# A decoder layer on one core: ten more chunks of the down projection by seven products, with the sums of their weights formed earlier and kept in DRAM

## The chip, the core and the metric

The kernel runs on one NeuronCore of a Trainium2 chip. The core's engines run side by side, each through its own queue in program order: PE multiplies matrices, DVE and ACT work elementwise, POOL here issues transfers and little else, SP issues the other transfers. A result goes from engine to engine by semaphores. SBUF is the memory on the core, PSUM holds PE's sums, DRAM is the large memory outside. The metric is the device time of one execution in microseconds; lower is better.

## The reference

One layer on 256 tokens of width 2048, in 32-bit floats:

```python
for l in range(DEPTH):
    h = rms_norm(x, attn_norm_g[l])
    proj = h @ w_in[l]
    q, k, v, p = jnp.split(proj, [ATTN_WIDTH, 2 * ATTN_WIDTH, 3 * ATTN_WIDTH], axis=-1)
    ...
    a = moba_attention(q, k, heads(v), rel_bias)
    m = multiscale_pool(p, pool_w[l], pool_scale[l])
    x = x + jnp.concatenate([a, m], axis=-1) @ w_out[l]
    x = x + conv_ffn(rms_norm(x, ffn_norm_g[l]), w_up[l], conv_w[l], conv_b[l], w_down[l])
```

Here `conv_ffn` multiplies by `w_up` (2048 x 11264), applies a causal convolution of width 3 to each column over the tokens, multiplies SiLU of the first half (the gate) with the second half (the value), and multiplies by `w_down` (5632 x 2048). The four large products, with `w_in` (2048 x 4096), `w_out` (2048 x 2048), `w_up` and `w_down`, are nearly all of the arithmetic.

## The kernel before, in words

**Weights and their two parts.** All weights come as a sequence of *chunks*, 128 partitions by 2048 columns, 1 MB each, in the order of their use: 24 chunks for the input projection's first part, 25 for its pooling part and the output projection, then three *thirds* of the feed-forward layer (8, 8 and 6 groups of 256 hidden columns). To keep 32-bit accuracy, a number is split into a high part, which PE multiplies at full rate, and a low part, the rest. A chunk is loaded by SP into one of four `raw` buffers (`load`, L112), ACT copies the high part into `wh` (L125, from chunk 51 on L151, one chunk further ahead), and DVE subtracts that from `raw` into `wl` (L126 or L157). A product of two matrices is then three matmuls: high by high, high by low, low by high. There are four `wh` and three `wl` buffers. When `wl` is made, the `raw` buffer is free and the chunk four further on is loaded into it (`release`, L189).

**Order of the work.** The program is a list of steps, one for each half chunk; the loop at L939 writes a step's instructions for all engines in turn. With the step that begins chunk c it first writes the splitting of chunk c + 2 (and ACT's copy of c + 3), then what was put off (`agenda`, filled by `later`; `deferred`), then the chunk's matmuls, and after a block's last matmul the evacuation of its sums. Each engine keeps this order.

**Output projection.** Eight blocks of 256 output columns, four steps (two chunks) each; the first two are mixed with the pooling weights. After a block, `residual` (L683) copies half of the sums by ACT, adds the other half by DVE (L511), adds the residual (L686) and sums squares (L691 on ACT, L692 on DVE); one step later `x2_split` makes the normalised input's two parts. After the last block, `sums2` forms the rows of mean squares, which go through DRAM on POOL's queue to be spread over the partitions. Loads of the residual `x2f` stand on SP's queue when `open_late` (L661) opens the second pool of buffers, four steps into this stage.

**Up projection.** In each third, each group has a gate block and a value block, two chunks each. After a block DVE evacuates it (L511, L767); with the next step come its convolution (L776 on ACT, L777 and L779 on DVE) and, for a value block, the product with the gate (L802). Two steps later the low part of the hidden values is made (L807), and for groups that use seven products `left_sums` (L812) forms four sums of the hidden values' quarters, split in their turn (ACT L821, DVE L822, two steps later). In the first third `x2_turn` also transposes the residual through DRAM.

**Down projection.** A chunk holds 256 hidden rows by 1024 output columns of `w_down`: a 2 x 2 matrix of blocks (128 by 512) on either side. `eight_products` takes eight products, 24 matmuls. `seven_products` uses the Strassen-Winograd scheme: seven products of sums of blocks, 21 matmuls, with the left side's sums from `left_sums` and the right side's four sums of weight blocks from `right_sums` (L163), which DVE forms in place in `raw` (L167 to L170) and ACT (L179) and DVE (L181) split into `th` and `tl`. Both halves of the output columns (`nb`) pass in turn. `SEVEN` (L55) says which groups of a third go by seven products: groups 1, 3 and 5 in the first two thirds, 1 and 3 in the last, 16 of 44 chunks.

## Time and profile before

| | |
|---|---|
| median of 3 runs | 998.84 us (998.66 to 999.5) |
| profiled execution | 999.07 us, span 997.3 us |
| granted TensorE clock | 1.000 |
| PE busy | 990.7 us, 99% |
| DVE busy | 802.1 us, 80% |
| ACT busy | 528.9 us, 53% |
| POOL busy | 61.4 us, 6% |
| moved by DMA | 210.34 MB, mean 211 GB/s |

The span runs from the first to the last instruction. Busy time of PE counts matmuls as they overlap, so it shows where PE had work and not how fast it went; the distance between the starts of two matmuls tells that. In groups of instructions a row has the line, engine, operation, the tiles written and read, the shapes and the count, and behind the bar the busy time in us and the mean of one in ns. In a timeline a row has the start and the duration in us, engine, line and tiles, and in brackets how long the engine was idle before it and what ended that.

### The profile page before, as it was taken

What the parts mean: (1) busy time and instruction counts of PE and PEld (TensorE: products, weight loads), DVE (VectorE), ACT (ScalarE), POOL (GpSimd) and SP (SyncE); (2) the same over time, 40 slices, a digit from 0 to 9 for tenths busy, and PEclk for the clock granted to TensorE, in tenths of its full rate; (3) what the DMA queues carried; (4) which work ended last, traced back from release to release, by engine and by line L of the source; (5) the groups of instructions that cost most, each with busy time, mean ns of one, the idle gap of its engine ahead of it and who ended that gap; (6) DMA issues with size and microseconds to landing.
All of it is one profiled execution on the core that took longest, in us unless ns stands there. A gap on an engine that the chain in (4) does not pass through costs nothing.

```text
span 997.3 us, 13236 instructions
## 1 busy us (share of the span) xinstructions
PE 990.7 (99%) x5306; PEld 856.8 (86%) x5306; DVE 802.1 (80%) x943; ACT 528.9 (53%) x560; POOL 61.4 (6%) x119
## 2 busy tenths in 40 slices
PE   9999999999999999999999999999999999999998
PEld 7888888898888888888888888888888888888886
DVE  6776858867779968789998778878999867877996
ACT  6554545446456555456544555555554545555641
POOL 0302232200003300000000000000000000000000
PEclk9999999999999999999999999999999999999999
DMA  9959685665558965554656555555455665555361
GB/s 351 316 208 291 233 259 195 206 261 199 195 178 284 302 218 180 193 191 166 215 207 217 206 188 192 190 197 205 163 199 186 219 235 180 192 191 208 130 237 55
DMA packets 36156, 210.34 MB, mean 211 GB/s; under 512 B 5288, under 2 KB 7720, under 8 KB 13184
## 3 DMA queue, kind: packets, MB, share of 16 engines
q1 hardware_dynamic: 31408, 197.58, 56.4%
q0 software_dynamic: 4688, 11.94, 4.2%
q8 instruction: 41, 0.67, 0.3%
q14 instruction: 19, 0.16, 0.0%
HBM read 201.23 MB, written 8.26 MB: 210 GB/s over the span
## 4 chain that ended last, share of the span: by engine, by line
PE 91%; issue 4%; DMA 3%; DVE 1%; POOL 1%; SPq 0%; ACT 0%; POOLq 0%; DVEq 0%
PE ps_feat L241 41%; PE ps_down L828 23%; PE ps_feat L243 20%; PE ps_val L219 4%; PE ps_tok L229 2%; DMA qT<-q1d 1%; DMA eT<-e3d 1%; DMA q0d<-q0x 1%; PE ps_pool L250 1%; DMA eT<-e0d 1%; DMA raw<-in_wts 0%; DVE wl L126 0%; POOL qT L441 0%; DMA e0d<-e0x 0%; PE ps_s L462 0%
## 5 line engine op out<-in xcount | busy, mean ns | idle before, releaser
L241 PE MATMUL ps_feat<-x2h,wh 128*128 128x512 f32 x1406 | 478.2, 389 | 0.0
L243 PE MATMUL ps_feat<-x2h,wl 128*128 128x256 f32 x1408 | 388.6, 276 | 0.0
L241 PEld LDWEIGHTS ps_feat<-x2h,wh 128*128 128x128 f32 x1406 | 263.9, 188 | 54.6
L157 DVE TENSOR_TENSOR wl<-raw,wh 128x2048 fp32r<-128x2048 f32 (+2 forms) x145 | 286.1, 1990 | 3.0 <-issue 3.0
L243 PEld LDWEIGHTS ps_feat<-x2h,wl 128*128 128x128 f32 x1408 | 264.3, 188 | 0.0
L151 ACT ACTIVATE wh<-raw 128x2048 fp32r<-128x2048 f32 (+2 forms) x145 | 241.3, 1677 | 39.6 <-PE ps_down L828 30.3
L828 PE MATMUL ps_down<-wh,hid 128*128 128x512 f32 x512 | 163.3, 389 | 0.0
L126 DVE TENSOR_TENSOR wl<-raw,wh 128x2048 fp32r<-128x2048 f32 (+3 forms) x60 | 119.6, 2000 | 49.6 <-ACT wh L125 40.9
L511 DVE TENSOR_TENSOR fs<-ps_feat,fs 128x512 f32<-128x512 f32 x52 | 35.9, 691 | 97.7 <-ACT fs L510 97.7
L828 PEld LDWEIGHTS ps_down<-wh,hid 128*128 128x128 f32 x512 | 96.1, 188 | 20.0
L125 ACT ACTIVATE wh<-raw 128x2048 fp32r<-128x2048 f32 (+3 forms) x60 | 99.9, 1682 | 10.8 <-DMA raw<-in_wts 7.5
L828 PE MATMUL ps_down<-wl,hid 128*128 128x512 f32 x256 | 99.6, 389 | 0.0
L241 PE MATMUL ps_feat<-cat,wh 128*128 128x512 f32 x256 | 87.3, 389 | 0.0
L229 PE MATMUL ps_tok<-wh,xh 128*128 128x512 f32 x256 | 80.0, 391 | 0.0
L510 ACT ACTIVATE fs<-ps_feat 128x512 f32<-128x512 f32 x52 | 31.0, 596 | 84.7 <-PE ps_feat L243 83.2
L243 PE MATMUL ps_feat<-cat,wl 128*128 128x256 f32 x256 | 70.7, 276 | 0.0
L179 ACT ACTIVATE th<-raw 128x1024 fp32r<-128x1024 f32 x32 | 34.0, 1063 | 51.3 <-DVE raw L168 46.0
L229 PEld LDWEIGHTS ps_tok<-wh,xh 128*128 128x128 f32 x256 | 48.0, 188 | 10.0
L828 PEld LDWEIGHTS ps_down<-wl,hid 128*128 128x128 f32 x256 | 48.1, 188 | 9.9
L241 PEld LDWEIGHTS ps_feat<-cat,wh 128*128 128x128 f32 x256 | 48.1, 188 | 9.8
L803 ACT ACTIVATE hid<-y 128x512 fp32r<-128x512 f32 x22 | 13.9, 633 | 76.7 <-DVE y L802 76.7
L229 PE MATMUL ps_tok<-wl,xh 128*128 128x512 f32 x128 | 49.8, 389 | 0.0
(196 smaller groups left out, 1076.0 us busy)
## 6 DMA issues: line engine op xcount, KB each, us to landing
raw<-in_wts SPq DMA_DIRECT2D x178, 1024.0 KB, 4.9
raw<-in_wts SPq DMA_DIRECT2D x4, 512.0 KB, 7.0
x2d<-x2x POOLq DMA_DIRECT2D x4, 512.0 KB, 6.3
x<-x2d POOLq DMA_DIRECT2D x32, 64.0 KB, 6.0
xboth<-in_xT SPq DMA_DIRECT2D x6, 256.0 KB, 10.0
out<-x SPq DMA_DIRECT2D x3, 512.0 KB, 3.9
x2f<-in_xT SPq DMA_DIRECT2D x1, 1024.0 KB, 8.7
x2f<-in_xT SPq DMA_DIRECT2D x1, 768.0 KB, 6.8
```

The source lines that it names most:

```text
L125: nc.scalar.activation(wh, w, AF.Copy)
L126: nc.vector.tensor_tensor(wl, w, wh.bitcast(F32), op=OP.subtract)
L151: nc.scalar.activation(w[:, lo:lo + n], raws[c][:, lo:lo + n], AF.Copy)
L157: nc.vector.tensor_tensor(wl[:, lo:lo + n], r[:, lo:lo + n], wh[:, lo:lo + n].bitcast(F32), op=OP.subtract)
L179: nc.scalar.activation(part(t[0]), part(r), AF.Copy)
L219: nc.tensor.matmul(ps[b][:, t, :], xh[:, k, a, ts], w[:, ws], start=False, stop=(k == KT - 1 and n == 2), skip_group_check=True)
L229: nc.tensor.matmul(ps[:, t, :], act[:, k0 + k, a, ts], w[:, ws], start=(first and k == 0 and n == 0), stop=(last and k == 1 and n == 2))
L241: nc.tensor.matmul(ps, wh[:, ws], act[:, k, :, :], start=(bool(first) and n == 0), stop=False, skip_group_check=True)
L243: nc.tensor.matmul(ps[:, S:], wl[:, ws], act[:, k, 0, :], start=False, stop=(last and n == len(ks) - 1), skip_group_check=True)
L510: nc.scalar.activation(dst, ps[:, :, S:], AF.Copy)
L511: nc.vector.tensor_tensor(dst, ps[:, :, :S], dst, op=OP.add)
L828: nc.tensor.matmul(ps, a, w, start=(first and n == 0), stop=(last and n == 2), skip_group_check=True)
```

## The change

Ten more chunks go by seven products: groups 1 to 5 in the first two thirds and 1 to 3 in the last, 26 of 44 (`SEVEN`). The right side's sums are no longer formed where they are used. For each of the 26 chunks the host lays out the blocks b22, b12, b11, b21 once more as an array `mix`. During the output projection (six) and the up projection (twenty), SP loads such a chunk into a `raw` buffer, `make` forms the four sums in place on DVE with three operations, and POOL stores the 1 MB to DRAM (`mixed`). The load that follows into that buffer is written two steps later (`later(2, load_next)`). In the down stage such a chunk then comes as two: a `sum` chunk, loaded from `mixed` (2048 columns), and a `rest` chunk with b11, b22 and b21 (1536 columns). Both are split like any other chunk, and the seven products fall into twelve matmuls (`seven_mixed`) and nine (`seven_rest`). `plan` lists the chunks in order and the places of the makes: in the output projection at chunks 40, 42, ... 50, in the up projection once per group. `th`, `tl` and their pieces are gone; the room goes to a fifth `raw` buffer (from `open_late` on) and to two more buffers for the left sums, which also hold the residual `x2f` now (four tiles, five loads). No arithmetic moves to the host, which only lays weights out.

```diff
-SEVEN = ((1, 3, 5), (1, 3, 5), (1, 3))
-TOFF, SOFF, SPAD = 32, 48, 64
+SEVEN = ((1, 2, 3, 4, 5), (1, 2, 3, 4, 5), (1, 2, 3))
+MAKES = (40, 42, 44, 46, 48, 50)
+PAIRS = ((2, 3, 4, 5, 6, 7), (0, 1, 2, 3, 4, 5, 6, 7), (0, 1, 2, 3, 4, 5))
+SOFF, SPAD = 32, 64
...
+def plan():
+
+    rows, makes = [(k, i) for i, k in enumerate(24 * ["tok"] + 25 * ["feat"])], list(MAKES)
+    n = t = 0
+    for (g0, g1), sevens, pairs in zip(THIRDS, SEVEN, PAIRS):
+        makes += [len(rows) + 4 * p + 3 for p in pairs]
...
+    mixed = [dram.tile([P, CH], F32, name=f"mixed{i}", tag=f"mixed{i}") for i in range(len(makes))]
+    order = [r for c in range(len(rows)) for r in [c] + [("make", i) for i, m in enumerate(makes) if m == c]]
+    del order[:4]
...
+        if isinstance(c, tuple):
+            src, n = mix[c[1]], CH
+        else:
+            kind, i = rows[c]
+            src, n = mixed[i] if kind == "sum" else wts[i], n or width(c)
         s = slice(lo, lo + n)
-        (queue or nc.sync).dma_start(raws[c][:, s], wts[c][:, s])
+        (queue or nc.sync).dma_start(raws[c][:, s], src[:, s])
...
-    def right_sums(r):
...
+    def make(i):
+
+        r = raws.pop(("make", i))
+        t3, t2, t4 = (r[:, k * 512:(k + 1) * 512] for k in (0, 2, 3))
+        nc.vector.tensor_tensor(r[:, :1024], r[:, :1024], r[:, 512:1536], op=OP.subtract)
+        nc.vector.tensor_tensor(t2, t3, t2, op=OP.add)
+        nc.vector.tensor_tensor(t4, t4, t2, op=OP.subtract)
+        nc.gpsimd.dma_start(mixed[i], r)
+        later(2, load_next)
...
+    def load_next():
+
+        if order:
+            c = order.pop(0)
...
             load(c)
...
-        for k0, k1 in ((0, 2), (2, 8), (8, KT)):
+        late["x2f"] = [block("x2f").rearrange("p (k t) -> p k t", t=S) for _ in range(4)]
+        for k0, k1 in ((0, 2), (2, 4), (4, 8), (8, 12), (12, KT)):
...
-    def seven_products(u, j, run, first, last):
...
+    def seven_mixed(u, j, run, first):
+
+        c = where[u][0]
+        t3, t1, t2, t4 = quarters(c)
+        del wparts[c]
+        s1, s2, s3 = (tuple(late["S", j][:, a, i, :] for a in range(2)) for i in range(3))
+        a22 = tuple(late["hid"][:, 2 * j + 1, a, P:] for a in range(2))
         p1, p5, p6, p7 = run["p"]
-        product(p5, s1, t1, first, last)
-        product(p6, s2, t2, first, last)
-        product(p7, s3, t3, first, last)
-        product(c1[0], a22, t4, (1, 0) in run["left"], False)
-        product(p1, a11, b11, first, last)
+        product(p5, s1, t1, first, False)
+        product(p6, s2, t2, first, False)
+        product(p7, s3, t3, first, False)
+        product(run["c"][1][0], a22, t4, (1, 0) in run["left"], False)
+
+    def seven_rest(u, j, run, first, last):
...
+        product(run["p"][0], a11, b11, first, last)
         product(c0[0], a12, b21, (0, 0) in run["left"], False)
         product(c0[1], s4, b22, (0, 1) in run["left"], False)
...
-            c, now[0] = u // 2 + 2, u
+            c, now[0] = starts[u] + 2, u
...
+            for i, m in enumerate(makes):
+                if m == c:
+                    make(i)
             for f in agenda.pop(u, ()):
                 f()
...
         if seven:
-            return [np.concatenate([b11, b12], axis=1), np.concatenate([b22, b21], axis=1)]
+            mix.append(np.concatenate([b22, b12, b11, b21], axis=1))
+            return [np.concatenate([b11, b22], axis=1), np.concatenate([b21, np.zeros_like(b21)], axis=1)]
```

Three places of DVE's queue show what moves (each row an instruction: line, operation, tile written from tiles read, size). The changed file's lines have other numbers: L159 and L187 are the low parts (L126 and L157 before), L195 to L197 the make, L533 an evacuation's add (L511), L788 the up block's scaling (L767), L828 the hidden values' low part (L807). First one block of the output projection, before:

```order
L511 TENSOR_TENSOR fs<-ps_feat,fs 128x512
L686 TENSOR_TENSOR x2f<-fs,x2f 128x512
L692 TENSOR_TENSOR sq_1799<-sq_1799,xs 128x512
L126 TENSOR_TENSOR wl<-raw,wh 128x2048
L702 SCALAR_TENSOR_TENSOR x2h<-x2f,pv,x2h 128x256 x2
L126 TENSOR_TENSOR wl<-raw,wh 128x2048
```

and now:

```order
L533 TENSOR_TENSOR fs<-ps_feat,fs 128x512
L707 TENSOR_TENSOR x2f<-fs,x2f 128x512
L713 TENSOR_TENSOR sq_1829<-sq_1829,xs 128x512
L159 TENSOR_TENSOR wl<-raw,wh 128x2048
L723 SCALAR_TENSOR_TENSOR x2h<-x2f,pv,x2h 128x256 x2
L159 TENSOR_TENSOR wl<-raw,wh 128x2048
L195 TENSOR_TENSOR raw<-raw 128x1024
L196 TENSOR_TENSOR raw<-raw 128x512
L197 TENSOR_TENSOR raw<-raw 128x512
```

The make's three operations stand behind the block's second low part and ahead of the next evacuation. Next the end of a gate block of the up projection, after a group with seven products, before:

```order
L157 TENSOR_TENSOR wl<-raw,wh 128x2048
L807 TENSOR_TENSOR hid<-y,hid 128x2x256
L816 TENSOR_TENSOR ls<-y 128x128
L817 TENSOR_TENSOR ls<-ls,y 128x128
L818 TENSOR_TENSOR ls<-y 128x128
L819 TENSOR_TENSOR ls<-y,ls 128x128
L511 TENSOR_TENSOR fs<-ps_feat,fs 128x512
L767 TENSOR_TENSOR u_1800<-fs,rrow_2552 128x2x256
L157 TENSOR_TENSOR wl<-raw,wh 128x2048
```

and now:

```order
L187 TENSOR_TENSOR wl<-raw,wh 128x2048
L195 TENSOR_TENSOR raw<-raw 128x1024
L196 TENSOR_TENSOR raw<-raw 128x512
L197 TENSOR_TENSOR raw<-raw 128x512
L828 TENSOR_TENSOR hid<-y,hid 128x2x256
L837 TENSOR_TENSOR ls<-y 128x128
L838 TENSOR_TENSOR ls<-ls,y 128x128
L839 TENSOR_TENSOR ls<-y 128x128
L840 TENSOR_TENSOR ls<-y,ls 128x128
L533 TENSOR_TENSOR fs<-ps_feat,fs 128x512
L788 TENSOR_TENSOR u_1830<-fs,rrow_2620 128x2x256
L187 TENSOR_TENSOR wl<-raw,wh 128x2048
```

Here the make stands ahead of the hidden values' low part and the left sums. Last the turn into the first third's down stage, before with one seven-product chunk:

```order
L802 TENSOR_TENSOR y<-y 128x512
L157 TENSOR_TENSOR wl<-raw,wh 128x512
L157 TENSOR_TENSOR wl<-raw,wh 128x1024
L167 TENSOR_TENSOR raw<-raw 128x512
L168 TENSOR_TENSOR raw<-raw 128x512
L169 TENSOR_TENSOR raw<-raw 128x512
L170 TENSOR_TENSOR raw<-raw 128x512
L181 TENSOR_TENSOR tl<-raw,th 128x1024
L181 TENSOR_TENSOR tl<-raw,th 128x2x512
L807 TENSOR_TENSOR hid<-y,hid 128x2x256
```

and now:

```order
L187 TENSOR_TENSOR wl<-raw,wh 128x1536
L798 SCALAR_TENSOR_TENSOR y<-u_1831,pv,y 128x256
L800 SCALAR_TENSOR_TENSOR y<-u_1831,pv,y 128x256
L798 SCALAR_TENSOR_TENSOR y<-u_1831,pv,y 128x256
L800 SCALAR_TENSOR_TENSOR y<-u_1831,pv,y 128x256
L823 TENSOR_TENSOR y<-y 128x512
L187 TENSOR_TENSOR wl<-raw,wh 128x2048
L828 TENSOR_TENSOR hid<-y,hid 128x2x256
L187 TENSOR_TENSOR wl<-raw,wh 128x1536
```

The sums and `tl` are gone from this place; between the convolution and the first products stand only low parts of whole chunks. In all, PE's queue holds 978 matmuls into `ps_down` where it held 1008.

More of the change, by code (lines that the diff above doesn't have):

```diff
@@ L83, in layer @@
 @with_exitstack
-def layer(ctx: ExitStack, tc: tile.TileContext, xT, wts, par, rel_d, ident_d, icnt_d, out):
+def layer(ctx: ExitStack, tc: tile.TileContext, xT, wts, mix, par, rel_d, ident_d, icnt_d, out):
     nc = tc.nc
@@ L184, in half @@
     def half(u):
-        parts = wparts[u // 2] if u % 2 == 0 else wparts.pop(u // 2)
-        return tuple(w[:, (u % 2) * HALF:(u % 2 + 1) * HALF] for w in parts)
+        c, k = where[u]
+        parts = wparts.pop(c) if k else wparts[c]
+        return tuple(w[:, k * HALF:(k + 1) * HALF] for w in parts)
     def release(c):
         raws.pop(c)
-        c += RAWS
-        if c < KT // 2:
-            load_xT(2 * c, 2 * c + 2)
-        if c < wts.shape[0]:
+        load_next()
+    def load_next():
+        if order:
+            c = order.pop(0)
+            if not isinstance(c, tuple) and c < KT // 2:
+                load_xT(2 * c, 2 * c + 2)
@@ L257, in feat_half @@
                [(slice(k * 256 + m * P, k * 256 + (m + 1) * P), k0 + k) for k in range(4)],
-               "apart" if first and m == 0 and u // 2 in AFTER_DOWN else first, last)
+               "apart" if first and m == 0 and rows[where[u][0]][1] in AFTER_DOWN else first, last)
     xh = keep.tile([P, KT, 2, S], F32R, name="xh", tag="h")
@@ L672, in open_late @@
             nc.gpsimd.memset(u[:, :, :2], 0.0)
+        load_next()
     def x2_tiles(k0, k1):
-        return late["x2f"][k0 // 8][:, k0 % 8:k0 % 8 + k1 - k0, :]
+        return late["x2f"][k0 // 4][:, k0 % 4:k0 % 4 + k1 - k0, :]
     def scratch(name):
@@ L680, in block @@
     def block(name, dt=F32):
-        return late["pool"].tile([P, SPAD + 1024], dt, name=name, tag="sums", bufs=3)[:, SOFF:SOFF + 1024]
+        return late["pool"].tile([P, SPAD + 1024], dt, name=name, tag="sums", bufs=5)[:, SOFF:SOFF + 1024]
     def residual(ps, g):
@@ L938, in layer @@
     assert n == 2 * wts.shape[0], (n, wts.shape)
+    starts = {}
+    for c, (kind, i) in enumerate(rows):
+        for k in range(1 if kind in ("sum", "rest") else 2):
+            where.append((c, k))
+        starts[len(where) - k - 1] = c
+    assert n == len(where), (n, len(where))
     for u in range(n):
@@ L998, in chunks @@
                 out += pair(w_down, 2 * (g0 + j), 1024 * nb, j in sevens)
-    return np.stack([np.concatenate(out[i:i + 2], axis=1) for i in range(0, len(out), 2)])
+    return np.stack([np.concatenate(out[i:i + 2], axis=1) for i in range(0, len(out), 2)]), np.stack(mix)
 def kernel(x, attn_norm_g, w_in, q_norm_g, k_norm_g, rel_bias, pool_w, pool_scale,
```

102 lines of the change are left out of this document (50 added, 52 removed).

## The prediction

> **What bounds the kernel now.** I read the page's first lines, then what PE waited for (engine, tile and line, what it waited for, us in all, times, longest), then the chain of waits (start, us, what).
>
> ```profile
> span 997.3 us, 13236 instructions
> PE 990.7 (99%) x5306; PEld 856.8 (86%) x5306; DVE 802.1 (80%) x943; ACT 528.9 (53%) x560; POOL 61.4 (6%) x119
> ```
>
> ```profile
> PE ps_val L210 <- ACT wh L125: 1.1, 2, 0.6
> PE ps_start L293 <- DVE ones L281: 1.1, 1, 1.1
> PE ps_av L498 <- DMA eT<-e3d: 0.4, 1, 0.4
> ```
>
> ```profile
> 459.96 82.98 PE ps_down L828 x366
> ```
>
> The median of the runs shown is 998.84 us; the profiled execution took 999.07, of which 997.3 is span, so a change of the span is taken as a change of the run. PE waits 2.6 us in all; none of it lies after 146 us. The last row is the first third's down projection: 366 matmuls of 512 columns in one piece, 82.98 / 366 = 0.2267 us each, without a wait. (A matmul's 389 ns in the groups is latency and overlaps its neighbour.) So PE sets the time, and every other engine matters only where it comes late to PE. How near they are to that is read from the timelines of DVE and PE. First the output projection, where columns are start, duration, engine and line, and the bracket is DVE's idle time and what ended it:
>
> ```profile
> 229.68 2.29 DVE L126 TENSOR_TENSOR wl<-raw,wh 128x2048 fp32r<-128x2048 f32 x1
> 232.15 0.69 DVE L511 TENSOR_TENSOR fs<-ps_feat,fs 128x512 f32<-128x512 f32 x1 [0.18 <-ACT fs L510]
> ...
> 275.67 0.69 DVE L511 TENSOR_TENSOR fs<-ps_feat,fs 128x512 f32<-128x512 f32 x1 [1.60 <-ACT fs L510]
> 277.85 0.69 DVE L692 TENSOR_TENSOR sq<-sq,xs 128x512 f32<-128x512 f32 x1 [0.76 <-ACT xs L691]
> 279.66 2.29 DVE L126 TENSOR_TENSOR wl<-raw,wh 128x2048 fp32r<-128x2048 f32 x1 [1.12 <-ACT wh L125]
> 282.66 2.29 DVE L126 TENSOR_TENSOR wl<-raw,wh 128x2048 fp32r<-128x2048 f32 x1
> 286.55 0.69 DVE L511 TENSOR_TENSOR fs<-ps_feat,fs 128x512 f32<-128x512 f32 x1 [1.60 <-ACT fs L510]
> ...
> 291.76 0.86 DVE L702 SCALAR_TENSOR_TENSOR x2h<-x2f,pv,x2h 128x256 fp32r<-128x256 f32 x2
> 292.55 2.27 DVE L126 TENSOR_TENSOR wl<-raw,wh 128x2048 fp32r<-128x2048 f32 x1
> ```
>
> and PE's timeline at the first up chunk:
>
> ```profile
> 285.71 0.39 PE L241 MATMUL ps_feat<-x2h,wh 128*128 128x512 f32 x1
> ...
> 286.05 0.39 PE L241 MATMUL ps_feat<-x2h,wh 128*128 128x512 f32 x1
> ```
>
> From 275.67 to 286.55 is one block of 256 output columns, whose weights are two chunks: 10.88 us, 5.44 a chunk (PE's pairs of a wide and a narrow matmul start 0.34 apart, 286.05 - 285.71, sixteen to a chunk). DVE's chain in it is 9.28 us, since 1.60 of the 10.88 is waiting for the block's end; the 0.76 and 1.12 are waits on ACT inside the chain and stay even when DVE is late. L126 makes a chunk's low part wl two chunks ahead: the one ending at 279.66 + 2.29 = 281.95 serves the chunk that PE starts at 285.71 (the first one reading x2h). DVE's lead is 3.76 us there, not the two chunks that the code suggests. The last one, 292.55 to 294.82, serves PE at 285.71 + 10.88 = 296.59: 1.77 us. The second place is the up projection, DVE's timeline over one pair of blocks with left sums and one without, then ACT's and PE's inside the first:
>
> ```profile
> 587.17 0.69 DVE L511 TENSOR_TENSOR fs<-ps_feat,fs 128x512 f32<-128x512 f32 x1 [3.23 <-ACT fs L510]
> 588.51 2.28 DVE L157 TENSOR_TENSOR wl<-raw,wh 128x2048 fp32r<-128x2048 f32 x1
> 590.71 0.48 DVE L777 SCALAR_TENSOR_TENSOR y<-u,pv,y 128x256 f32<-128x256 f32 x1
> ...
> 593.27 2.29 DVE L157 TENSOR_TENSOR wl<-raw,wh 128x2048 fp32r<-128x2048 f32 x1
> ...
> 598.27 0.69 DVE L511 TENSOR_TENSOR fs<-ps_feat,fs 128x512 f32<-128x512 f32 x1 [1.19 <-ACT fs L510]
> 599.61 2.28 DVE L157 TENSOR_TENSOR wl<-raw,wh 128x2048 fp32r<-128x2048 f32 x1
> ...
> 608.93 0.69 DVE L511 TENSOR_TENSOR fs<-ps_feat,fs 128x512 f32<-128x512 f32 x1 [2.40 <-ACT fs L510]
> ...
> 619.87 0.69 DVE L511 TENSOR_TENSOR fs<-ps_feat,fs 128x512 f32<-128x512 f32 x1 [1.96 <-ACT fs L510]
> ...
> 630.69 0.69 DVE L511 TENSOR_TENSOR fs<-ps_feat,fs 128x512 f32<-128x512 f32 x1 [3.16 <-ACT fs L510]
> ```
>
> ```profile
> 604.90 1.92 ACT L151 ACTIVATE wh<-raw 128x2048 fp32r<-128x2048 f32 x1
> ```
>
> ```profile
> 608.10 0.39 PE L241 MATMUL ps_feat<-x2h,wh 128*128 128x512 f32 x1
> ```
>
> A pair takes 608.93 - 587.17 = 21.76 us. The low part ending at 599.61 + 2.28 = 601.89 is needed by the chunk that starts at 608.10: a lead of 6.2 us. Evacuating a block takes DVE 588.51 - 587.17 = 1.34, a low part 2.20, the convolution and the product with the gate 593.27 - 590.71 = 2.56.
>
> **The change part by part: what is removed.** Ten more down chunks go from 24 products to 21: 30 matmuls x 0.2267 = **6.8 us of PE time**, the only gain that can reach the end. The 26 seven-product chunks also lose DVE work in the down stage (four 512-wide sums, three-piece lows), but PE waits for none of it today, so that is worth nothing there.
>
> **What is added to DVE.** Each of 26 makes is one 1024-wide and two 512-wide tensor operations, like these in the groups by line and shape (busy us, mean ns):
>
> ```profile
> L181 DVE TENSOR_TENSOR tl<-raw,th 128x1024 fp32r<-128x1024 f32 x32 | 39.0, 1222 | 0.0
> L170 DVE TENSOR_TENSOR raw<-raw 128x512 f32<-128x512 f32 x16 | 11.1, 693 | 0.5
> ```
>
> 1.22 + 0.69 + 0.69 = 2.6, less some overlap of successive starts: 2.56 us. In the output projection six makes stand in six successive blocks, right behind the second low part and ahead of the block's evacuation, the next low part queued behind that. The first falls between 231.97 and the add at 232.15, so that add moves to about 234.5, 2.35 late. Each later block has 1.60 idle to give: 2.56 - 1.60 = 0.96 more lateness. After six: 2.35 + 5 x 0.96 = 7.15. Low parts come that much later, and nothing can be made up before the chunk of 296.59, whose lead was 1.77, about 1.9 with PE's first high product done meanwhile. **PE stalls 7.15 - 1.9 = 5.2 us** there, in four or five waits: under 0.5 at the third make, about 1 at each of the next two, near 3 at the last, where the sums of squares (up to 291.76) stand ahead of the low part.
>
> In an up pair the make stands in the gate block, between the second low part and the left sums. With left sums, the gate block's 1.19 idle is a wait for ACT that follows the sums and stays. Of the value block's 2.40 idle, ACT's own order (activation from 604.90 for 1.92, then the copy of 0.6) lets the next add start at 607.35 instead of 608.93, so 1.58 can be used. 2.56 - 1.58 = 0.98 later per pair. Without left sums all of 1.96 and 3.16 - 0.82 = 2.34 can be used: 1.96 + 2.34 - 2.56 = 1.7 is recovered. First and second thirds now have five pairs with sums and a make: the low part after the fifth make is 2.56 + 4 x 0.98 = 6.5 late against 6.2, a stall of 0.3. Lateness of 5 x 0.98 - 0.3 = 4.6, less 1.7 in the last pair, goes on into the down stage: 2.9. There PE reaches the second sum chunk after (24 + 12 + 9) x 0.2267 = 10.2 us, while DVE needs 8.4 for that chunk's low part (ACT's copy 0.6, evacuation 1.34, three quarters of a low part 1.65, convolution and product 2.56, low part 2.20): a lead of 1.8, a stall of 2.9 - 1.8 = 1.1. So 1.4 in each of two thirds; the last third has three such pairs, 2.9 - 1.7 = 1.2 late, within 1.8: none. DVE in all: **5.2 + 2.8 = 8.0 us**. Bounds: 0, if I mistake a lead by the size of the lateness, and 10.5 if ACT adds half a microsecond of waiting per pair or block.
>
> **What is added to DMA.** 26 loads of the sums' operands, 26 stores, 26 loads of the sums, at 1.05 MB each, less a quarter of 26 loads. From the stretches of the span and from the page's list of transfers:
>
> ```profile
> 20.00:50.00 30.00, 30.00 (x134) 24.86 (x133) 22.61 (x21) 19.03 (x19) 7.71 (x13) 1.00 0.94 334
> 85.00:95.00 10.00, 10.00 (x46) 8.26 (x45) 5.20 (x3) 2.14 (x3) 0.56 (x1) 1.00 1.00 354
> 247.00:258.00 11.00, 11.00 (x67) 9.77 (x66) 7.48 (x8) 5.79 (x7) 0.00 (x0) 1.00 0.53 191
> 390.00:412.00 22.00, 22.00 (x131) 19.55 (x130) 17.36 (x21) 11.90 (x13) 0.00 (x0) 1.00 0.57 194
> ```
>
> ```profile
> raw<-in_wts SPq DMA_DIRECT2D x178, 1024.0 KB, 4.9
> x2d<-x2x POOLq DMA_DIRECT2D x4, 512.0 KB, 6.3
> ```
>
> The last two columns of a stretch are the share of the 16 engines and GB/s; projection and up stage stand at 191 and 194. The queue's best stretch is 354 GB/s at full share; 334 was had at 0.94. In the up stage a pair asks for six transfers, 6.3 MB in 21.76 us, 289 GB/s: hidden. In the down stage five seven-product chunks ask for 1.835 MB in 4.76 us, 385 GB/s, for 23.8 us: 0.74 MB more than 354 gives, against five raw buffers that are full when it begins; I take 0, and 0.74 MB / 354 = 2.1 us per half if that cover is gone. The first load after a make goes into its buffer and waits on SP for the store, with all later loads behind it: the make ends some 5 us into its chunk, a store of twice 512 KB takes 6 to 10 us, the load 4.9, so it lands 16 to 20 us in, and ACT needs it at four chunks, 21.8: 0, or the 2 us by which it would miss. In the output projection a block asks for two weight chunks, a mix and a store: 4.19 MB. At 354 that is 11.84 us, just DVE's new 9.28 + 2.56; at 334 it is 12.55, 0.7 more in each of five blocks, 3.5. The sixth store also stands on POOL's queue ahead of the row of mean squares, for which DVE waits in the first up block. I take 1.2 between 0 and 3.5, nearer to the row with the higher share.
>
> The Trainium skill (Trainium Kernel Development and Optimization, Key Constraints) says that transfers issued from SP, ACT and POOL share the same 16 engines, so putting the store on POOL buys no bandwidth; DMA: Bandwidth & Descriptors, Specifications, gives a core's share of HBM as about 358 GB/s. The row of 354 agrees. By 358 a block needs 11.7 us, the 1.2 would be 0 and the sum 1000.0.
>
> Costed at nothing: ACT and DVE in a run of seven-product chunks (1.75 parts each, 3.4 and 3.9 us in PE's 4.76; each microsecond over would be paid 26 times), the five instead of three residual loads (the same bytes, four chunks early), a fifth raw buffer, and POOL's issue time (POOL is otherwise idle).
>
> Sum: -6.8 + 8.0 + 1.2 = +2.4 on the profiled 999.07, so 1001.5 for it and 998.84 + 2.4 = **1001.2 us** for the median.
>
> **Rivals.** *DVE's lateness is absorbed* (the other side). DVE is idle a fifth of the time, and leads of 3.8 to 6.2 us are real; if the makes mostly fill waits, PE keeps the whole 6.8: 992.0. Against it stand the 1.60 of idle per block and 2.56 of make; it decides if DVE's addition per block is under 1.8 us. *DMA bounds the output projection*: 3.5 instead of 1.2, and the row late by the 3 us that a 1.05 MB store takes at 354: 1001.2 + 2.3 + 3.0 = 1006.5. For it: reads and writes mixed at that rate appear nowhere in the trace. *PE resumes in a slower step.* After its wait at 145 us the feature pairs run 0.35 apart instead of 0.34, and stay so to 167 us:
>
> ```profile
> 145.41 0.67 PE L498 MATMUL ps_av<-eT,v 128*128 128x256 f32 x2 [0.41 <-DMA eT<-e3d]
> ...
> 147.80 0.40 PE L241 MATMUL ps_feat<-xh,wh 128*128 128x512 f32 x1
> ...
> 165.47 0.40 PE L241 MATMUL ps_feat<-xh,wh 128*128 128x512 f32 x1
> ```
>
> There are 50 pairs between the last two rows, (165.47 - 147.80) / 50 = 0.3534 each. At 0.0134 us a pair a third of 32 chunks loses 6.9; since DVE gains the same time, the 1.4 of stalls goes: +5.5, 1006.7. It can be set off by any of the new stalls, but most starts of such a run fall back to 0.34 within three pairs. *The change does not do what it says*: the program holds 30 matmuls less, so only a hidden wait on the stored sums could undo it; they are stored tens of microseconds before they are loaded: about 999.
>
> **How the numbers follow.** Likeliest, with 0.47: the forecast, by itself 996.5 to 1004 (0 to 10.5 of DVE waits does not all belong to it; below 996.5 it is the first rival). Absorbed 0.23, DMA 0.13, slower step 0.13, no effect 0.04. A change under 0.2%, 2 us, can't be told from none. Faster: the 0.23 and 0.02 of the forecast's low end, 0.25. Within: 0.21 of the forecast and 0.04, 0.25. Slower: 0.24 + 0.13 + 0.13 = 0.50. The range 993 to 1007.5 leaves out half of the absorbed case and the ends of two others.
>
> **What would show it.** Right: ps_down matmuls down from 1008 to 978; PE waits "ps_feat <- DVE wl" of 4 to 6 us between 250 and 300 us, the longest at the third up chunk; two waits of about a microsecond around the turn from up to down in the first two thirds, none in the last; no waits inside a run of five seven-product chunks. DVE idle in the output projection only on ACT. Wrong: PE's waits total under 2 us (absorbed), or DVE's low parts there wait for ACT, and ACT for raw loads (DMA), or pairs are 0.3535 apart for whole chunks (slower step).

## The result and the profile after

| | before | after |
|---|---|---|
| median of the runs, us | 998.93 | 1009.85 |
| lowest to highest, us | 998.66 to 999.50 | 1008.48 to 1016.39 |
| the profiled execution, us | 999.07 | 1016.39 |

The ratio is 1.0123, with a 95% interval of 1.0083 to 1.0164: the change makes the kernel about 11 us slower. The forecast was 1001.2 us, in a range up to 1007.5. The profiled execution is the longest of those shown (two further ones took 1008.85 and 1014.65 us), so the same kernel was profiled once more (the last but one of the experiments, 1009.48 us); that one stands for the usual run. Of the runs below, four single executions of 1032 to 3715 us, far over all others of their kernels, are left out.

First where the time lies. The stages are cut at the first matmul of each on PE's timeline, which for the first up and down stage of the profile after are

```profile
288.09 0.40 PE L263 MATMUL ps_feat<-x2h,wh 128*128 128x512 f32 x1
...
482.91 0.40 PE L849 MATMUL ps_down<-wh,hid 128*128 128x512 f32 x1
```

| stage, us | before | after, profiled | after, once more |
|---|---|---|---|
| up to the output projection | 192.88 | 193.69 | 193.08 |
| output projection | 92.83 | 94.40 | 94.01 |
| first third, up | 174.08 | 194.82 | 188.75 |
| first third, down | 82.99 | 80.24 | 80.27 |
| second third, up | 174.12 | 174.35 | 174.40 |
| second third, down | 82.98 | 81.01 | 81.07 |
| last third, up | 130.61 | 130.61 | 130.61 |
| last third, down | 62.75 | 61.39 | 61.39 |

The three down stages together win 6.1 of the 6.8 us that were forecast. The output projection loses 1.6 and 1.2, the second third's up stage 0.2 and 0.3. All the rest is one stage: the first third's up projection is 20.7 us longer in the profiled execution and 14.7 in the usual one. The page after, and what PE waited for:

```profile
span 1014.6 us, 13410 instructions
...
PE 999.8 (99%) x5276; PEld 858.5 (85%) x5276; DVE 846.1 (83%) x960; ACT 540.2 (53%) x543; POOL 75.0 (7%) x145
```

```profile
PE ps_feat L263 <- DVE x2h L723: 3.5, 1, 3.5
PE ps_feat L265 <- DVE wl L187: 2.4, 1, 2.4
PE ps_feat L263 <- DVE fs L533: 1.6, 1, 1.6
...
PE ps_down L849 <- DVE wl L187: 0.5, 1, 0.5
PE ps_feat L265 <- DVE wl L159: 0.4, 2, 0.2
```

PE is at 99% as before, and its new waits come to 8.4 us. They can't be 20.7. Three things have to be told apart, and each has its rows. **The waits**, from DVE's timeline:

```profile
270.57 0.68 DVE L533 TENSOR_TENSOR fs<-ps_feat,fs 128x512 f32<-128x512 f32 x1
...
282.33 0.68 DVE L533 TENSOR_TENSOR fs<-ps_feat,fs 128x512 f32<-128x512 f32 x1
...
293.04 1.22 DVE L195 TENSOR_TENSOR raw<-raw 128x1024 f32<-128x1024 f32 x1 [1.24 <-DMA raw<-in_mix]
...
315.20 0.40 DVE L391 TENSOR_SCALAR rs<-row 128x256 f32<-128x256 f32 x1 [7.96 <-DMA row<-row_d]
```

Blocks are evacuated 282.33 - 270.57 = 11.76 us apart instead of 10.88: the makes are where the prediction put them. The sixth make waits for its operands, whose load is the 10.55 in the chain below. SP's queue shows why that load was issued late (queue, line, what it waited for, us, times, longest):

```profile
SPq L150 <- DMA mixed<-raw: 61.8, 6, 12.3
```

From 230 to 330 us it stood 61.8 us for stores that were still reading raw buffers. Then DVE stands for 7.96 us before line 391, which reads the row of mean squares. While it stands it evacuates no block, and PE, with no free accumulator, waits for fs at 319 us and for the next low part at 322.

```profile
282.39 10.55 DMA raw<-in_mix
...
307.18 8.00 DMA row<-row_d
...
483.07 80.25 PE ps_down L849 x354
```

**Half pace behind a wait.** PE's timeline, wide matmuls only, and the stretches of the span (columns as in the prediction, the third from the right is the granted clock):

```profile
297.36 0.40 PE L263 MATMUL ps_feat<-x2h,wh 128*128 128x512 f32 x1
...
301.35 0.79 PE L263 MATMUL ps_feat<-x2h,wh 128*128 128x512 f32 x1 [3.47 <-DVE x2h L723]
...
302.15 0.63 PE L263 MATMUL ps_feat<-x2h,wh 128*128 128x512 f32 x1
...
302.79 0.63 PE L263 MATMUL ps_feat<-x2h,wh 128*128 128x512 f32 x1
...
306.63 0.63 PE L263 MATMUL ps_feat<-x2h,wh 128*128 128x512 f32 x1
...
307.27 0.40 PE L263 MATMUL ps_feat<-x2h,wh 128*128 128x512 f32 x1
```

```profile
296.00:304.00 8.00, 4.53 (x19) 3.63 (x19) 6.96 (x16) 5.06 (x6) 1.05 (x2) 0.78 0.98 353
...
313.00:324.00 11.00, 6.92 (x34) 5.52 (x34) 6.96 (x12) 5.49 (x7) 4.35 (x8) 0.86 0.67 239
...
340.00:440.00 100.00, 100.00 (x567) 86.35 (x566) 88.61 (x112) 52.38 (x56) 11.40 (x21) 1.00 0.79 285
```

After the wait that ends at 301.35 the pairs start 0.64 apart, not 0.34, up to 307.27; the granted clock is 0.78 in the stretch from 296 to 304 us, and 0.86 from 313 to 324 us, behind the next waits. There are 16 pairs of this kind in the stage, 4.8 us above 0.34.

**The step of 0.3534.** The row for 340 to 440 us has no wait and a clock of 1.00, but holds 567 matmuls of feature pairs where 100 us at 0.34 hold 588. Where it begins:

```profile
264.42 0.39 PE L263 MATMUL ps_feat<-cat,wh 128*128 128x512 f32 x1
...
264.76 0.39 PE L263 MATMUL ps_feat<-cat,wh 128*128 128x512 f32 x1
...
265.35 0.39 PE L263 MATMUL ps_feat<-cat,wh 128*128 128x512 f32 x1
...
265.70 0.40 PE L263 MATMUL ps_feat<-cat,wh 128*128 128x512 f32 x1
```

One pair takes 0.59 (the low part made from 262.78 to 265.07 is a quarter of a microsecond late), and from there pairs are 0.35 apart, through the whole up projection to 482 us: 488 pairs in the first up third, 6.5 us.

So 20.7 = 9.4 of waits, counted on the pairs (what those around a wait take over 0.34), 4.8 at half pace, 6.5 of longer step. The same three sums for the usual run are 11.4, 2.4 and 0.9, together 14.7.

### The profile page after: what moved, and what is told of

Its sections match the earlier page's. It is cut to its first block, busy times and chain, and to the rows that moved or that the text cites. A ratio compares the mean times of both kernels' runs of the same rounds, so it can differ in the third digit from the quotient of the medians.

```text
span 1014.6 us, 13410 instructions
## 1 busy us (share of the span) xinstructions
PE 999.8 (99%) x5276; PEld 858.5 (85%) x5276; DVE 846.1 (83%) x960; ACT 540.2 (53%) x543; POOL 75.0 (7%) x145
## 4 chain that ended last, share of the span: by engine, by line
PE 71%; DVE 14%; issue 6%; DMA 5%; ACT 2%; POOL 1%; SPq 0%; DVEq 0%; POOLq 0%; ACTq 0%
PE ps_feat L263 29%; PE ps_down L849 21%; PE ps_feat L265 15%; DVE wl L187 5%; PE ps_val L241 4%; PE ps_tok L251 2%; DVE y L800 1%; DVE fs L533 1%; DVE y L798 1%; DMA raw<-in_mix 1%; DVE raw L195 1%; ACT wh L181 1%; DVE u L788 1%; DVE wl L159 1%; DMA qT<-q1d 1%
## 5 line engine op out<-in xcount | busy, mean ns | idle before, releaser
L263 PE MATMUL ps_feat<-x2h,wh 128*128 128x512 f32 x1406 | 490.3, 395 | 5.1 <-DVE x2h L723 3.5
L187 DVE TENSOR_TENSOR wl<-raw,wh 128x2048 fp32r<-128x2048 f32 (+1 forms) x155 | 339.2, 2195 | 18.7 <-PE ps_down L849 7.1
L181 ACT ACTIVATE wh<-raw 128x2048 fp32r<-128x2048 f32 (+1 forms) x155 | 285.3, 1844 | 79.0 <-PE ps_down L849 57.2
L159 DVE TENSOR_TENSOR wl<-raw,wh 128x2048 fp32r<-128x2048 f32 (+3 forms) x60 | 119.5, 1999 | 50.0 <-ACT wh L158 38.6
L849 PE MATMUL ps_down<-wh,hid 128*128 128x512 f32 x444 | 142.4, 389 | 0.0
L849 PEld LDWEIGHTS ps_down<-wh,hid 128*128 128x128 f32 x444 | 83.3, 188 | 17.3
L849 PE MATMUL ps_down<-wl,hid 128*128 128x512 f32 x222 | 86.4, 389 | 0.0
L533 DVE TENSOR_TENSOR fs<-ps_feat,fs 128x512 f32<-128x512 f32 x52 | 35.8, 689 | 49.7 <-ACT fs L532 49.7
L849 PE MATMUL ps_down<-wh,sums 128*128 128x512 f32 x208 | 69.2, 389 | 0.0
L198 POOL DMA_DIRECT2D mixed<-raw x26 | 13.9, 536 | 666.7 <-DVE raw L197 643.2
L797 ACT ACTIVATE y<-u,pv 128x256 f32<-128x256 f32 x88 | 47.6, 590 | 5.5 <-DVE u L788 5.5
L811 ACT ACTIVATE y<-y 128x512 f32<-128x512 f32 x22 | 13.9, 634 | 68.6 <-DVE y L800 68.6
```

The costliest lines, as they stand in the source:

```text
L159: nc.vector.tensor_tensor(wl, w, wh.bitcast(F32), op=OP.subtract)
L181: nc.scalar.activation(w, raws[c][:, :width(c)], AF.Copy)
L187: nc.vector.tensor_tensor(wl, raws[c][:, :width(c)], wh.bitcast(F32), op=OP.subtract)
L198: nc.gpsimd.dma_start(mixed[i], r)
L263: nc.tensor.matmul(ps, wh[:, ws], act[:, k, :, :], start=(bool(first) and n == 0), stop=False, skip_group_check=True)
L533: nc.vector.tensor_tensor(dst, ps[:, :, :S], dst, op=OP.add)
```

## The experiments

My theory after the two traces was that the loss is made at the turn from the output to the up projection: the stores make the sixth mix load and the row late, which gives the waits and the half pace, and a first short wait sets the longer step. Its rivals were DVE's own lateness, and the longer step alone. Each kernel is the changed one with one edit, compared with runs of the kernel before on the same chip.

### The makes one block earlier

```diff
-MAKES = (40, 42, 44, 46, 48, 50)
+MAKES = (38, 40, 42, 44, 46, 48)
```

> The same six makes in the output projection, each one block (two chunks) earlier, so that none stands in the block before the turn to the up projection. Theory (the loss is made at the turn: sixth mix load 10.6 us in landing, 1 KB row 5.5 us and row of mean squares 8.0 us behind the sixth store, three PE waits of 7.5 us and 20 us of clock at 0.66): the row lands within 3 us of its need, the three waits shrink to under 2 us together, no stretch of the up stage under a clock of 0.9; 993 to 1001 us, the upper end if feature pairs still run 0.3534 apart through the first up third. Rival A (six makes are too much for DVE in this stage wherever they stand): lateness is the same, PE's waits stay near 7 us, 1006 to 1010. Rival B (only the slower step matters): waits go and the time falls by no more than 4 us, 1005 or more.

Measured 1009.58 us, ratio 1.0110 (1.0094 to 1.0127), where rival A put it. The row is still late. The stretch from the issue of the row's first transfer until the row has landed, before, after, and here (the last two columns are the share of the 16 DMA engines and GB/s):

```profile
292.10:298.40 6.30, 6.30 (x39) 5.61 (x38) 6.08 (x5) 2.82 (x2) 1.10 (x2) 1.00 0.44 89
```

```profile
301.20:315.20 14.00, 13.85 (x63) 11.91 (x64) 6.05 (x5) 2.88 (x2) 1.60 (x3) 0.78 0.95 339
```

```profile
301.70:314.10 12.40, 12.40 (x75) 10.95 (x74) 6.06 (x6) 2.81 (x2) 1.62 (x3) 1.00 1.00 342
```

The row takes 6.3 us before, 14.0 after and 12.4 here, although the last store was issued at 287.34, 14 us ahead of it, and had landed at 297.02. A free block is not enough, and that part of the theory fell. DVE's lateness stays as well, as rival A has it: the output projection is 5.3 us longer than in the kernel before. The rows show what goes with the row's lateness: in that stretch the DMA engines are busy 0.44 of the time before, at 89 GB/s, and 0.95 and 1.00 with the makes. What fills them here is no store. The transfers issued from 297.07 to 314.1 us are, besides 0.5 MB and the row itself, loads of weights on SP's queue:

```profile
raw<-in_wts SPq DMA_DIRECT2D x5, 1024.0 KB, 7.4
...
row_d<-qrow POOLq DMA_DIRECT2D x1, 1.0 KB, 4.7
```

The first three of these loads are issued within a microsecond from 297.07, just when the store has landed. In the kernel before, SP issues no load from 285.4 to 294.8 us, and two in the stretch of the row.

### Makes that store nothing

```diff
-            src, n = mixed[i] if kind == "sum" else wts[i], n or width(c)
+            src, n = (mixed[i] if i >= len(MAKES) else mix[i]) if kind == "sum" else wts[i], n or width(c)
...
-        nc.gpsimd.dma_start(mixed[i], r)
+        if i >= len(MAKES):
+            nc.gpsimd.dma_start(mixed[i], r)
```

> The six makes of the output projection compute their sums but store nothing, and their six sums chunks load the unsummed operands instead (the same bytes; these products are not the reference's). Theory (the stores hold raw buffers and SP's queue, and the row waits behind the sixth): SP waits on no store before 330 us, the mix loads land in under 7 us, the row in under 7 us from the first issue to the landing as in the kernel before (1.6 and 4.4), waits at the turn under 2 us and the clock stays 1.0; 993 to 1001. Rival (DVE's 2.56 us a block against 1.60 idle): low parts still late by 4 to 7 us, PE waits of 4 to 6 us remain around 290 us; 1003 to 1010.

Measured 1005.67 us, ratio 1.0071 (1.0053 to 1.0090). PE's waits from 250 to 335 us, and the stretch of the row:

```profile
PE ps_feat L264 <- DVE x2h L724: 2.3, 1, 2.3
PE ps_feat L266 <- DVE wl L159: 1.2, 2, 0.6
```

```profile
300.20:306.60 6.40, 6.24 (x26) 5.32 (x27) 6.09 (x6) 2.80 (x2) 1.15 (x3) 0.73 0.46 108
```

Without stores the row takes 6.3 us again, at a DMA share of 0.46, and DVE waits 0.3 for it: the stores make the row late, as the theory has it. But this is not the whole loss. What is left is DVE's lateness (the operands are still loaded): 3.5 us of waits, 4.8 counted on the pairs, the longest at the third up chunk, as the rival says and as the prediction had it. Behind that wait of 2.3 us five pairs run at half pace (1.5 us), and behind those the step of 0.3534 holds for 477 pairs (6.4 us). The time is over the range that the theory gave and within the rival's.

### Makes that add nothing

```diff
-        nc.vector.tensor_tensor(r[:, :1024], r[:, :1024], r[:, 512:1536], op=OP.subtract)
-        nc.vector.tensor_tensor(t2, t3, t2, op=OP.add)
-        nc.vector.tensor_tensor(t4, t4, t2, op=OP.subtract)
+        if i >= len(MAKES):
+            nc.vector.tensor_tensor(r[:, :1024], r[:, :1024], r[:, 512:1536], op=OP.subtract)
+            nc.vector.tensor_tensor(t2, t3, t2, op=OP.add)
+            nc.vector.tensor_tensor(t4, t4, t2, op=OP.subtract)
```

> The six makes of the output projection load and store but add nothing on DVE (these six chunks' products are not the reference's). Theory (stores and loads make the turn late): DVE keeps its idle time of 1.6 us a block, yet SP still waits about 12 us for stores, the row still takes over 10 us from its first issue to the landing, and the wait for it at the turn stays; 1000 to 1007. Rival (DVE): no new wait of PE, pairs 0.34 apart; 992 to 994.

Measured 1003.05 us, ratio 1.0054 (1.0032 to 1.0075), in the range of the theory.

```profile
PE ps_feat L264 <- DVE fs L534: 4.1, 1, 4.1
PE ps_feat L266 <- DVE wl L187: 2.1, 1, 2.1
```

```profile
291.60:306.60 15.00, 14.98 (x89) 13.02 (x87) 6.34 (x6) 5.38 (x3) 1.63 (x3) 1.00 0.99 388
```

The output projection takes 92.84 us, no more than before, and no low part is late in it. The transfers alone make the row take 14.9 us, at a share of 0.99, and cost 6.2 us of waits and 2.4 of half pace; the first up third is 10.7 us longer, 1.1 of it behind the fifth pair with left sums and a make. So by waits and half pace loads and stores, which the prediction priced at 1.2, are the larger of the two causes: 9.6 us (the 10.7 less the 1.1), against 6.3 for DVE's sums alone (4.8 of waits, 1.5 of half pace). They do not simply add up, since both make PE late for the same chunks. By the times of the runs it is the other way round, 1003.05 against 1005.67: in the profile without stores the longer step held for 477 pairs behind DVE's wait, here for 62 of the first up third.

### The row's transfers issued from ACT

```diff
-        nc.gpsimd.dma_start(d, q[:, 0, :])
+        nc.scalar.dma_start(d, q[:, 0, :])
...
-        nc.gpsimd.dma_start(late["row"], bass.AP(tensor=d.tensor, offset=d.offset, ap=[[0, P], [1, S]]))
+        nc.scalar.dma_start(late["row"], bass.AP(tensor=d.tensor, offset=d.offset, ap=[[0, P], [1, S]]))
```

> The changed kernel with the two small transfers of the row of mean squares issued from ACT instead of POOL, so that they no longer stand in the queue that holds the stores. Theory (the row is late because its queue delivers the 1 MB stores first): the two land in about 1.6 and 4.4 us as in the kernel before, DVE waits under 1 us for the row instead of 8.0, PE's wait for the evacuated block at 319 us goes and with it the second stretch at a clock of 0.66; waits of 2 to 4 us from DVE's own lateness stay: 1002 to 1007. Rival (the 16 engines are busy with 1 MB pieces whatever the queue): 5 and 8 us again, no gain, 1008 or more, and ACT held up besides.

Measured 1010.57 us, ratio 1.0123 (1.0106 to 1.0140): the rival. The page's list of transfers has for them

```profile
row<-row_d ACTq DMA_DIRECT2D x1, 128.0 KB, 7.7
row_d<-qrow ACTq DMA_DIRECT2D x1, 1.0 KB, 6.0
```

and the stretch

```profile
299.00:313.40 14.40, 6.84 (x29) 5.91 (x30) 6.07 (x6) 6.32 (x5) 0.00 (x0) 0.64 0.92 336
```

On a queue with no store in it, 1 KB takes 6.0 us and 128 KB 7.7, as in the queue with the stores (5.7 and 8.0). So it is not the place in POOL's queue, as the prediction had it. What all the late rows have in common, here and with the makes one block earlier, is the load on the engines that all queues share. ACT meanwhile holds up its own products until the first transfer has landed, and PE waits 9.8 us for x2h:

```profile
PE ps_feat L263 <- DVE x2h L723: 9.8, 1, 9.8
```

The Trainium skill (DMA: Bandwidth & Descriptors, Issuing engines are not separate DMA queues) says that transfers of the three issuing engines interleave on the same 16 engines and that another issuer saves only issue time; the run agrees.

### A split first matmul at every block

```diff
-AFTER_DOWN = (97, 145)
+AFTER_DOWN = (*range(37, 81, 2), 97, 145)
```

> The changed kernel, with the first wide matmul of every block of 37 to 79 issued as two of 256 columns, as the kernel already does at the first block behind each down stage. Theory (a short wait shifts PE into a step of 0.3534 us a pair that stays until something shifts it back, 0.0134 us a pair over some 530 pairs, and the split first matmul shifts it back): pairs return to 0.34 within each block; about 7 us less than the changed kernel, 1001 to 1005 us, with the three waits of 7.5 us at the turn still there or 2 us longer, since DVE gains less time. Rival (the step is not PE's own but set by something beside it, such as DMA or DVE traffic): pairs stay 0.353 apart and the time stays at 1008 to 1012.

Measured 1015.55 us, ratio 1.0165 (1.0148 to 1.0182), the opposite of the theory. The split pair itself takes 0.35 to 0.36 us, but pairs start 0.3533 apart in every block from 220 to 297 and from 332 to 479 us. Only two of the splits, at 220.11 and 332.49 us, stand in a run at 0.34 without a wait, and behind both the longer step begins. The 18 others of these blocks stand within the longer step, and none ends it, as the theory had hoped. Between 301 and 332 us, behind waits at the turn, pairs return to 0.34, through two splits that themselves stand at waits. So a split seems to set the longer step here, on two cases. That also speaks against the rival, since the edit leaves DMA and DVE their work. In the kernel before and the changed one the split at the first block behind a down stage is followed by 0.34. What differs there is open.

### Fewer makes, and makes elsewhere

No makes in the output projection:

```diff
-SEVEN = ((1, 2, 3, 4, 5), (1, 2, 3, 4, 5), (1, 2, 3))
-MAKES = (40, 42, 44, 46, 48, 50)
+SEVEN = ((1, 3, 5), (1, 2, 3, 4), (1, 2, 3))
+MAKES = ()
```

> No makes in the output projection, twenty in the up stages only, and so twenty seven-product chunks (6, 8, 6) instead of 26: 12 matmuls of 0.2267 us less than the kernel before, 2.7 us. Theory (all of the loss comes from the output projection's makes, the up stages' makes cost PE at most 0.5 us a third): output projection 92.8 us, no clock under 0.9 after 285 us, 995 to 997.5. Rival (lateness in the up stages sets off the slower step, 0.0134 us a pair, or waits of 1.4 us a third): 998 to 1003.

Measured 995.95 us, ratio **0.9975 (0.9964 to 0.9987)**, faster than both kernels and in the range of the theory. PE waits for nothing behind 150 us; these are all its waits:

```profile
PE ps_start L315 <- DVE ones L303: 1.1, 1, 1.1
PE ps_av L520 <- DMA eT<-e3d: 0.6, 1, 0.6
```

The stages are 92.83, 174.08, 174.13 and 130.60 us, those of the kernel before, and the 12 matmuls saved arrive whole: 998.62 - 2.7 = 995.9.

Four makes, the last two blocks free: MAKES = (40, 42, 44, 46) and SEVEN = ((1, 2, 3, 4, 5), (1, 2, 3, 4), (1, 2, 3)).

> Four makes in the output projection, none in its last two blocks, and 24 seven-product chunks (10, 8, 6): 24 matmuls, 5.4 us, less than the kernel before. By the idle of 1.6 us a block, four makes leave DVE 2.35 + 3 x 0.96 = 5.2 us late and two free blocks give 3.2 back; the last store is issued 23 us ahead of the row. Theory (it is the makes nearest the turn that cost): waits under 1 us in the projection and at the turn, the row in under 7 us, 993 to 997. Rival (any short wait is enough to set the slower step): waits as small, but pairs 0.3534 apart for most of the first up third, 998 to 1001. Rival (stores and loads stay late for several blocks): row late again, 1001 or more.

Measured 1000.98 us, ratio 1.0024 (1.0013 to 1.0034), against the theory; the sign of the last rival, a late row, is there. The row takes 9.5 us from its issue 24 us behind the last store, at a DMA share of 0.66, and in the first up third PE waits for low parts four times, 3.8 us in all counted on the pairs: at 309 us after DVE has waited 3.5 for the row, and at 398, 420 and 443 us, where five pairs of blocks have left sums and a make.

All 26 kept, spread: MAKES = (11, 18, 37, 40, 42, 44).

> All 26 chunks kept, the six early makes spread: two in the token projections (behind the low parts of chunks 11 and 18, where DVE idles 3 to 6 us), one behind chunk 37, three in the output projection's fourth to sixth last blocks. Theory (the loss needs the makes packed against the turn): no wait over 0.5 us from 142 us to the end of the first up third, row in under 7 us, 992 to 995. Rival (each make costs where it stands, by the loads that it delays in a ring of four buffers): new waits of PE for high parts or raw loads before 142 us, 997 to 1003.

Measured 1002.81 us, ratio 1.0032 (1.0006 to 1.0058); the times lie in two groups, 997.8 to 998.4 and 1005.1 to 1007.7, with one of 1000.5 between. The profiled execution is of the first: the output projection takes 93.11 us, the row's two transfers 1.6 and 4.3, the first up third 174.58. But the two makes in the token projections delay all that follows: the next stage begins at 145.84 us instead of 141.37 (141.1 to 143.6 in the other runs). So these two cost where they stand, as the rival says, and the theory holds for the rest. The rival's mechanism is not seen: no wait for high parts or raw loads, but one of 2.6 us for ACT's line 473, which itself waited 3.0 for 128-KB transfers of q through DRAM. Again it is small transfers that come late. The distance of the groups, 7 to 8 us, is about a third at 0.3534 (6.9); no profile of the second group shows it.

Four makes at the front: MAKES = (37, 38, 40, 42), SEVEN as in the run with four.

> Four makes at the front of the output projection (behind chunks 37, 38, 40, 42), 24 seven-product chunks (10, 8, 6): 24 matmuls, 5.4 us, less than the kernel before. Theory: DVE has four blocks without a make to come back (4 x 1.6 us), the last store is issued about 45 us ahead of the row, which lands in 1.6 and 4.4 us; no wait in the projection or at the turn, at most 1.5 us of waits in the first up third from five left sums with a make: 993 to 996, or 7 us more where one of these waits sets the step of 0.3534 early in the third. Rival (any make in the projection leaves the raw ring late up to the turn): row over 5 us again, 998 to 1003.

Measured 997.06 us, ratio 0.9990 (0.9979 to 1.0001). The row is on time, at the share of before:

```profile
292.90:299.30 6.40, 6.40 (x39) 5.69 (x38) 6.25 (x6) 2.85 (x2) 1.10 (x3) 1.00 0.45 99
```

Of 5.4 us saved 4.8 are lost to short waits: 2.0 in the projection (waits of 0.8 and 0.2 for low parts, and 33 pairs at 0.3534 between them), 1.9 in the first up third, and 0.9 at the turn into its down stage. Ahead of the projection this profile is 1.2 us shorter than that of the kernel before.

Two makes at the front: MAKES = (37, 40), SEVEN = ((1, 3, 5), (1, 2, 3, 4, 5), (1, 2, 3)).

> Two makes at the front of the output projection (behind chunks 37 and 40), 22 seven-product chunks (6, 10, 6): 18 matmuls, 4.1 us, less than the kernel before. Theory: no wait of PE from 142 us to the end of the first up third, where only three blocks have left sums; at most 0.5 us at the second third's turn: 994.5 to 995.5, 1 to 1.4 us under the kernel with none in the projection (995.95). Rival (the gain is lost to a wait with a slower step behind it in the second third): 995.5 to 1000.

Measured 996.76 us, ratio 0.9986 (0.9977 to 0.9995). The projection and the first up third take 92.83 and 174.08. One pair of 0.62 at 694.6 us, behind the second third's fifth pair with left sums and a make, sets the step of 0.3534 for the rest of that stage: the stage is 1.1 us longer, as the rival has it. The span also ends 5.2 us behind PE's last matmul instead of 4.1, since the last transfer takes 3.1 us to land and not 2.1.

Two makes at the front, four pairs at most in a third: SEVEN = ((1, 3, 5), (1, 2, 3, 4), (1, 2, 3, 4)).

> As the run with two early makes, 22 seven-product chunks, but divided 6, 8, 8: no third has more than four pairs of blocks with left sums and a make. 18 matmuls, 4.1 us, less than the kernel before. Theory (DVE's lateness grows by 0.98 us for each such pair and reaches its lead with the fifth, and one wait of 0.3 us is enough to set the slower step): no wait of PE behind 142 us, no pair at 0.3534 from 210 us on, the three up stages at 174.1, 174.1 and 130.6 us, and 994.0 to 995.0. Rival (the last third, with six pairs only, has no room for a fourth): a wait in it or at its turn, with up to 2 us of slower step, 995 to 997.

Measured 999.22 us, ratio 1.0008 (0.9999 to 1.0017). In the up stages the theory holds: 174.08, 174.12 and 130.61 us, no wait and no pair at 0.3534. But the time lies over the ranges of both the theory and the rival. The last third's down stage takes the gain back:

```profile
PE ps_down L849 <- DVE wl L187: 1.6, 1, 1.6
...
PE ps_down L849 <- DVE sa L892: 0.4, 1, 0.4
```

The first of these waits is at the turn, the second where the other half of the output columns begins. Counted on the distances of its matmuls PE loses 3.3 us in this stage, and the run ends 7.4 us behind PE's last matmul instead of 5.8; on DVE's timeline the last sums of products run from 986.1 to 991.1 us, right ahead of the last additions, which before come after 3.9 us of idle. The last third has only two pairs without left sums to come back, and its chunks are the last of the program.

### The changed kernel once more

> The changed kernel once more, unchanged, for a second profile of it. Theory (each wait of PE inside a run of feature pairs starts the step of 0.3534 in about one case of three, so runs differ by up to 7 us per third): about the same three waits of 7.5 us at the turn and 10 to 16 pairs at 0.64 us, but another stretch at 0.3534; 1007 to 1017. Rival (the step follows from the program): the same stretch from 265 to 482 us again and 1015 to 1017.

One run, 1009.48 us.

```profile
PE ps_feat L263 <- DVE fs L533: 3.4, 1, 3.4
PE ps_feat L263 <- DVE x2h L723: 2.3, 1, 2.3
PE ps_feat L265 <- DVE wl L187: 2.1, 1, 2.1
```

```profile
313.00:324.00 11.00, 5.48 (x20) 4.13 (x19) 8.86 (x13) 7.29 (x9) 4.75 (x9) 0.69 0.76 284
...
340.00:440.00 100.00, 100.00 (x590) 88.48 (x589) 89.77 (x114) 54.12 (x58) 10.46 (x20) 1.00 0.81 290
```

The same waits at the turn and 8 pairs at half pace, fewer than foreseen, but 590 matmuls from 340 to 440 us: the step of 0.3534 begins only at 453 us, behind a wait of 0.7, and costs 0.9. So the step does not follow from the program alone. Counted on PE's timelines of the changed kernel and of all these variants but the one with the splits, 14 of 42 waits within feature pairs at 0.34 were followed by 0.3534, and 5 of 10 waits within 0.3534 ended it. The least of the 14 is a pair of 0.343 us, 3 ns late (at 395.3 us with four makes at the front), behind which 63 pairs stay at 0.3534.

## Why the prediction was wrong, step by step

- **Removed, 6.8 us.** Right: 6.1 in the down stages, and the rest is the forecast wait at the second third's turn.
- **DVE in the output projection, 5.2 us.** Right in place and mechanism, and nearly in size. Alone (no stores) it costs 4.8 us of waits counted on the pairs, the longest at the third up chunk. What ends that wait is x2h's second half, not the low part behind it.
- **DVE in the thirds, 1.4 + 1.4 + 0.** Right to some tenths. Behind the fifth pair with left sums and a make 0.3 was forecast: in the second third PE loses 0.17 to 0.28 there in the nine profiles that have a fifth one, and nothing with four. At the turn 1.1 was forecast: the second down stage is 0.8 longer than the first one, which loses nothing in the changed kernel's two profiles and 0.8 to 0.9 in three others (the row issued from ACT, spread, four at the front). The last third loses nothing.
- **DMA, 1.2 between 0 and 3.5.** This is the step that failed. "The sixth store also stands on POOL's queue ahead of the row" named the right victim and the wrong cause, and gave it no more than 3 us even in the rival. I priced each transfer by bandwidth over a block of the output projection, with 354 GB/s as the most. Neither holds: without the sums that stage is no longer than before (92.84 us), and the stretch of the row moved 388 GB/s, so that the 358 quoted beside it is no bound in this case either. The cost lies at the turn. A store holds a raw buffer, SP's queue stands behind it (61.8 us in six waits from 230 to 330 us), and when it is let go the loads that it held come together, just when the kernel before has its ebb. With the makes one block earlier these loads alone, with no store under way, filled the engines. In the changed kernel's crowd 1 KB and 128 KB took 14.0 us instead of 6.3. Alone (no sums) this costs 9.6 us of the first up third in place of 1.2; the list of waits has 6.2 of it, and 2.4 is half pace. "0, or the 2 us by which it would miss" for the first load behind a make was wrong in the same way: the load next behind it was the next make's operands, 10.55 us in landing where I took 4.9.
- **Left out: the half pace behind a wait.** 16 pairs and 4.8 us in the profiled execution, 8 and 2.4 in the usual one. No row of the kernel before showed it: in the page's slices its clock is full throughout.
- **The rival of the longer step, with 0.13.** It happened, in the profiled execution for 549 pairs. The sentence that "most starts of such a run fall back to 0.34 within three pairs" holds for a single wait (28 of 42). I did not raise it to the number of waits: with six or seven waits, one in three each, a stretch at 0.3534 is the rule and only its length is left to chance. Its side effect was as foretold: the profiled execution has no wait behind the first third's fifth such pair.
- **The range** ended 2.3 us under the median. It held each term's bounds, but no term for what a wait costs beyond its length.

## What to carry to other kernels

Price a wait of PE by what follows it too: here 2.3 us of waiting cost 1.5 more at half pace, and any wait had one chance in three of 4% on all feature pairs up to the next one. A DMA that waits in a loading ring does not only move bytes; it holds a buffer and lets the loads behind it bunch, so look for the small transfer on the critical path that today travels in the ebb, and leave room between the last large store and that transfer (here 24 us were too little and 34 enough). And count room on an engine per stretch between two deadlines: in the second third four pairs with left sums and a make fitted and a fifth did not, and a saving of 2.7 us taken whole beat savings of 4.1 to 6.8 us taken with waits.

## What the runs showed of the hardware

- **Half pace.** Behind waits that came to 2.3 us or more within a few pairs, 4 to 8 pairs started 0.64 apart; behind waits up to 1.3 us none did, and the granted clock stayed 1.00 there. The Trainium skill (TensorE: Matmul & The Clock Gate, HAM oscillation — how this bites in real kernels) warns of pauses above about 3.4 us; here less was enough, one wait of 2.25 us in the run without stores.
- **The longer step.** Two spacings of the same pair, 0.34 and 0.3534, both at clock 1.00, each stable for hundreds of pairs; waits change the one into the other without a rule that these runs show, once behind a pair only 3 ns late, and the longer one began at both splits that stood in a run at 0.34 without a wait. What it is in PE stays open.
- **Small transfers in a crowd.** While the row travelled, 1 KB landed after 1.6 us at DMA shares of 0.42 to 0.49 (seven profiles), after 2.8 at 0.66 (one), and after 4.7 to 7.3 us at 0.91 to 1.00 (six), from POOL's queue and from ACT's alike.
